# Decay-argument matmuls on 128 rows, and the C-B diagonal in one VectorE instruction

## The chip, the cores and the metric

The kernel runs on one core of a Trainium2 chip. The metric is the device time of one execution in microseconds (us). The profile shows the engines TensorE (PE for matmuls, PEld for the loads of their stationary operand), VectorE (DVE), ScalarE (ACT), GpSimd (POOL) and SyncE (SP), whose queue issues all DMAs here.

## The reference

One layer of a hybrid mixer over 2048 latent tokens of width 1024, with 256 context tokens as a prefix. What matters here is the state-space (SSD) group: 24 heads of 64 channels in 4 groups of 6 heads, a state of 128, chunks of 128 tokens, scanned in both directions.

```python
def ssd_chunked(x, dt, A, B, C, h0):
    ...
    xc = (x * dt[..., None]).reshape(bsz, nc, CHUNK, g, r, p)
    a = (dt * A).reshape(bsz, nc, CHUNK, g, r).transpose(0, 3, 4, 1, 2)
    a_cum = jnp.cumsum(a, axis=-1)
    lmat = jnp.exp(segsum(a))          # exp(a_cum[l] - a_cum[s]) for s <= l
    cb = jnp.einsum('bclgn,bcsgn->bgcls', cc, bc)
    y_diag = jnp.einsum('bgcls,bgrcls,bcsgrp->bclgrp', cb, lmat, xc)
    ...
    y_off = jnp.einsum('bclgn,bcgrpn,bgrcl->bclgrp', cc, prev_states, jnp.exp(a_cum))
    y = (y_diag + y_off).reshape(bsz, length, g, r, p)
...
y = y_f + flip(y_b) + d_skip.astype(f32).reshape(g, r)[:, :, None] * xs
gated = y.reshape(bsz, length, g, r * p) * jax.nn.silu(zs.astype(f32)).reshape(bsz, length, g, r * p)
gated = gated * lax.rsqrt(jnp.mean(gated * gated, axis=-1, keepdims=True) + EPS)
out = gated.reshape(bsz, length, D_SSD).astype(zs.dtype) * norm_w
```

## The kernel before

Projections, convolutions, the context scan, the backward scan and the Fourier group come first; they write their results to DRAM. The last stage, which the change is in, then makes the output. It runs over 64 units u: a chunk c of 128 tokens (16 of them) and a group g of 6 heads (4 of them). A unit has six steps, called for different units in one loop turn.

- s1 loads and makes the decay weights. For each direction dr, the exponent of all 6 heads comes from a matmul (L965) of a stationary tile l, which holds 12 rows of log dt minus cumulated decay (6 heads, a high and a low part) and 2 rows of ones, with a moving tile r, which holds 12 rows that select a head and 2 rows of the cumulated decay. These 14 rows start at partition 0 for dr = 0 and at 32 for dr = 1. The output parg has 128 x 384 elements, for three heads; there are two halves, h2 = 0 and 1. VectorE merges the two directions with a mask (copy_predicated, L967), ScalarE takes exp into w (L969), and VectorE multiplies w by C-B (cb, L970). A parg tile has two PSUM buffers.
- The matmul pcb (L947) gives C-B for the group; ScalarE copies it to cb. VectorE takes its diagonal: times the identity (cbi, L951), then a sum along the row (cbd, L953), and from it the scale dsc (L956) of the term that ScalarE makes in six instructions (xd, L1012). pcb shares one PSUM buffer with pn.
- s2 loads the states and makes the off-chunk output (pyo, L1005 to L1007), from high and low parts sh and sl; s3 advances the forward state hf (pst, L1031 to L1033, and L1036, L1037).
- s4 multiplies x by w (py, L1046, 64 output columns a head) and adds ts by transposes into the same PSUM tile (L1049); s5 makes the group's norm (pn, L1062, and L1065 to L1071); s6 multiplies by the output weights (po, L1105 to L1107) and, for the last group of a chunk, makes the residual and the final norm.

All engines have queues in order. The order of the instructions is set by a scheduler that simulates the program with costs of its own; it need not be the order of the source. Two tiles r (rt) take turns, and three tiles l (lt). Their constant rows are written once, before the stage; per unit SP loads the 2 rows of cumulated decay of r and the 12 rows of l, for each direction.

Of the kernel before, what the change touches and what calls it, by code (L numbers as in the profile page):

```python
# [9 lines left out]
F32 = mybir.dt.float32  # L10
F32R = mybir.dt.float32r
U8 = mybir.dt.uint8
AF = mybir.ActivationFunctionType
ALU = mybir.AluOpType
AX = mybir.AxisListType
# [3 lines left out]
P = 128  # L19
# [9 lines left out]
HG = 6  # L29
# [20 lines left out]
def mixer_layer(ctx: ExitStack, tc: tile.TileContext, A: dict, out: bass.AP, taps=None):  # L50
    nc = tc.nc
    mm = nc.tensor.matmul
# [9 lines left out]
    def load(dst, src):  # L62
        return nc.sync.dma_start(out=dst, in_=src).ins
# [3 lines left out]
    def copy(dst, src):  # L67
        return nc.scalar.activation(dst, src, AF.Copy).ins  # L68
# [21 lines left out]
    q_d = scratch("q_d", [2, W2, SEQ], F32R)  # L90
# [807 lines left out]
    msk32 = wa1.tile([P, HG, P], F32, name="st1", tag="w")[:, 0]  # L898
    load(msk32, A["msk"])
    nc.vector.tensor_copy(out=msk, in_=msk32)  # L900
    LR = 46
    rt = [wa1.tile([LR, HG * P], F32R, name=f"rt{i}", bufs=1) for i in range(2)]
    lt = [wa1.tile([LR, P], F32R, name=f"lt{i}", bufs=1) for i in range(3)]
    for t in rt:
        st1 = wa1.tile([P, HG, P], F32, name="st1", tag="w")
        load(st1[:LR], A["rrows"].rearrange("r (h w) -> r h w", w=P))
        copy(t, st1[:LR].rearrange("r h w -> r (h w)"))
    for t in lt:
        nc.vector.tensor_copy(out=t, in_=ones[:LR, :])

    for n in range(4):
        out_weights(n, lambda sh: W["p"].tile(sh, F32, name="wo", tag="raw", bufs=1), 1)
# [10 lines left out]
    def s1(u):  # L923
        c, g = divmod(u, G)
        d = units[u] = {}
        if g == 0:
            sml = wa1.tile([P, 4, W2], F32, name="sml4", tag="sml")
            load(sml, sm_d[c])
        else:
            sml = units[u - 1]["sml"]  # L930
        d["sml"] = sml
        r, l = rt[u % 2], lt[u % 3]
        cs = slice(c * P, c * P + P)
        for dr in range(2):
            hsl = slice(dr * H + g * HG, dr * H + (g + 1) * HG)
            load(r[32 * dr + 12:32 * dr + 14, :].rearrange("o (h w) -> o h w", w=P).bitcast(F32),
                 cum_d[:, hsl, cs].bitcast(F32))
            for s in range(2):
                load(l[32 * dr + 6 * s:32 * dr + 6 * s + 6, :].bitcast(F32), q_d[s, hsl, cs].bitcast(F32))
        bc = wa1.tile([P, 2, P], F32, name="bc", tag="bc", bufs=2)  # L940
        load(bc, bcT_d[c, :, g])
        d["bc"] = bc
        chl = wa1.tile([P, 2, P], F32R, name="chl", tag="chl")
        load(chl[:].bitcast(F32), chl_d[c, :, g].bitcast(F32))
        d["chl"] = chl
        pcb = ps.tile([P, P], F32, name="pcb", tag="misc", bufs=1)
        mm(pcb, bc[:, 0], bc[:, 1], start=True, stop=True)  # L947
        cb = wa1.tile([P, P], F32, name="cb", tag="cb")
        copy(cb, pcb)
        cbi = wa1.tile([P, P], F32, name="cbi", tag="cbi", bufs=1)  # L950
        nc.vector.tensor_tensor(out=cbi, in0=cb, in1=ident, op=ALU.mult)  # L951
        cbd = wa1.tile([P, 1], F32, name="cbd", tag="cbd")
        nc.vector.tensor_reduce(out=cbd, in_=cbi, axis=AX.X, op=ALU.add)  # L953
        dsc = wa1.tile([P, HG], F32, name="dsc", tag="dsc")
        hs = slice(g * HG, (g + 1) * HG)
        nc.vector.scalar_tensor_tensor(out=dsc, in0=sml[:, 3, H + g * HG:H + (g + 1) * HG], scalar=cbd[:, 0:1],  # L956
                                       in1=dsk[:, hs], op0=ALU.mult, op1=ALU.add)
        d["dsc"] = dsc
        w = wa1.tile([P, HG, P], F32, name="w", tag="w")
        for h2 in range(2):  # L960
            cols = slice(384 * h2, 384 * h2 + 384)
            pa = []
            for dr in range(2):
                po = ps.tile([P, 3, P], F32, name="parg", tag="arg", bufs=2)
                mm(po, l[32 * dr:32 * dr + 14, :], r[32 * dr:32 * dr + 14, cols], start=True, stop=True)  # L965
                pa.append(po)
            nc.vector.copy_predicated(out=pa[0], mask=msk[:].unsqueeze(1).broadcast_to([P, 3, P]), data=pa[1])  # L967
            with tc.issue_after(pre2):
                d["exp"] = nc.scalar.activation(w[:, 3 * h2:3 * h2 + 3], pa[0], AF.Exp).ins  # L969
        nc.vector.tensor_tensor(out=w, in0=w, in1=cb[:].unsqueeze(1).broadcast_to([P, HG, P]), op=ALU.mult)  # L970
        d["w"] = w
# [225 lines left out]
def shape_constants():  # L1197
    f = lambda a: np.ascontiguousarray(a, dtype=np.float32)
    K = {}
    i = np.arange(P)  # L1200
    K["ident"] = f(np.eye(P))
    K["sel"] = f(np.tile(np.eye(32)[:, :2], (4, 1)))
    K["i2"] = f(np.concatenate([np.eye(2 * H), np.eye(2 * H)], axis=0))
    K["ones"] = f(np.ones((P, P)))
    K["triu"] = f(i[:, None] <= i[None, :])
    K["tril"] = f(i[:, None] >= i[None, :])
    K["msk"] = f(i[None, :] < i[:, None])
    rr = np.zeros((46, HG * P))
    for base in (0, 32):
        for s in range(2):  # L1210
            for h in range(HG):
                rr[base + 6 * s + h, h * P:(h + 1) * P] = 1.0
    K["rrows"] = f(rr)
    n1 = np.arange(P)
    m1 = np.zeros((P, P))
    for k1 in range(64):
        t, k1l = divmod(k1, 4)
        m1[:, 2 * k1l * 16 + t] = np.cos(2 * np.pi * ((k1 * n1) % P) / P)
        m1[:, (2 * k1l + 1) * 16 + t] = -np.sin(2 * np.pi * ((k1 * n1) % P) / P)
    m1[:, 16] = np.cos(np.pi * n1)  # L1220
    K["dft1"] = f(m1)
    scale = 1.0 / math.sqrt(SEQ * 64.0)
    n2 = np.arange(16)
    k2 = np.arange(16)
    tw = np.zeros((16, 8, 16, 2, 16, 4))
    for t in range(16):
        for k1l in range(4):
            k1 = 4 * t + k1l
            th = 2 * np.pi * ((n2[:, None] * (k1 + P * k2[None, :])) % SEQ) / SEQ
            tw[t, 2 * k1l, :, 0, :, k1l] = np.cos(th)  # L1230
            tw[t, 2 * k1l, :, 1, :, k1l] = -np.sin(th)
            if k1 > 0:
                tw[t, 2 * k1l + 1, :, 0, :, k1l] = np.sin(th)
                tw[t, 2 * k1l + 1, :, 1, :, k1l] = np.cos(th)
    K["tw"] = f((tw * scale).transpose(0, 2, 1, 3, 4, 5).reshape(16, P, P).transpose(1, 0, 2))
    t64 = np.zeros((8, 16, 2, 16))
    th = 2 * np.pi * ((n2[:, None] * (64 + P * k2[None, :])) % SEQ) / SEQ
    t64[1, :, 0, :] = np.cos(th)
    t64[1, :, 1, :] = -np.sin(th)
    K["tw64"] = f((t64 * scale).transpose(1, 0, 2, 3).reshape(P, 32))  # L1240
    j = np.arange(64)
    th = 2 * np.pi * ((j[:, None] * j[None, :]) % 64) / 64
    for name, m in (("c64", np.cos(th)), ("s64", np.sin(th))):
        b = np.zeros((P, P))
        b[:64, :64] = m
        b[64:, 64:] = m
        K[name] = f(b)
    return K
# [15 lines left out]
```

## Time and profile before

| | us |
|---|---|
| Median of 3 runs | 1965.88 |
| Lowest and highest | 1959.27, 1967.3 |
| Span of the profiled execution, first to last instruction | 1965.1 |
| PE matmul busy in it | 1885.8 |
| DVE busy | 1478.9 |
| ACT busy | 890.0 |
| POOL busy | 809.4 |

The profile gives the profiled execution's span, and no time beside it; the span is 0.8 us under the median of the runs. Times of the trace count from the start of the span. Busy shares are averages over stages with different limits, so the stage from about 1215 us to the end is read by itself.

### The profile page before, as it was taken

The numbers are of one execution on the slowest core, as the hardware profiler recorded it, in microseconds if no ns is written. First come the engines' busy times: TensorE is split into PE (matmuls) and PEld (weight loads), VectorE is DVE, ScalarE is ACT, GpSimd is POOL, SyncE is SP. The second block draws the span as 40 slices with busy tenths as digits, with TensorE's granted clock in tenths as the row PEclk, the third lists the DMA queues.
The fourth block names the chain that finished last, engine by engine and source line by source line (L and its number), as shares of the span: only waits on it lengthen the run. The fifth ranks groups of instructions, "written<-read, shape, count | busy, mean of one in ns | idle before, by whom it ended". The sixth has DMA issues, their size and how long they took to land.

```text
span 1965.1 us, 27142 instructions
## 1 busy us (share of the span) xinstructions
PE 1885.8 (96%) x9136; PEld 1499.5 (76%) x9136; DVE 1478.9 (75%) x2083; ACT 890.0 (45%) x2008; POOL 809.4 (41%) x635
## 2 busy tenths in 40 slices
PE   6999999999999999999889999999999999999998
PEld 2799988878888788888677787667777677777776
DVE  3743298998988995338896136998999899999885
ACT  2631144444444443442332433665565555555653
POOL 1321021110201211035573224776777677777663
PEclk8999999999999999999999998879999999999999
DMA  7332132322423323355777547543343333334331
GB/s 267 143 96 77 35 107 60 113 83 66 121 70 89 113 79 101 104 162 189 259 260 235 193 133 230 177 148 118 117 123 115 112 111 120 117 109 129 119 119 37
DMA packets 233132, 253.12 MB, mean 129 GB/s; under 512 B 23269, under 2 KB 194245, under 8 KB 232482
## 3 DMA queue, kind: packets, MB, share of 16 engines
q1 hardware_dynamic: 232994, 251.39, 41.0%
q8 instruction: 73, 1.20, 0.3%
q14 instruction: 65, 0.53, 0.1%
HBM read 165.31 MB, written 86.02 MB: 128 GB/s over the span
## 4 chain that ended last, share of the span: by engine, by line
PE 61%; DVE 23%; DMA 4%; ACT 4%; issue 4%; POOL 3%; SPq 0%; DVEq 0%; ACTq 0%; POOLq 0%
DVE acc L434 10%; PE pj L170 8%; PE pj L169 8%; PE pj L171 8%; PE po L1105 4%; PE po L1107 4%; PE po L1106 4%; PE parg L965 3%; PE py L1046 2%; ACT xd L1012 2%; PE pj L381 2%; PE pj L380 2%; PE pj L379 2%; DVE xl L72 1%; DMA hb_d<-hs 1%
## 5 line engine op out<-in xcount | busy, mean ns | idle before, releaser
L434 DVE SCALAR_TENSOR_TENSOR acc<-img,c_convw,acc 128x1024 f32<-128x1024 f32 x320 | 464.0, 1457 | 59.0 <-ACT acc L431 48.9
L169 PE MATMUL pj<-hh,wh 128*128 128x512 f32 x1152 | 453.1, 397 | 1.2 <-DVE hs L673 1.2
L170 PE MATMUL pj<-hl,wh 128*128 128x512 f32 x1152 | 454.0, 394 | 0.0
L171 PE MATMUL pj<-hh,wl 128*128 128x512 f32 x1152 | 453.1, 393 | 0.0
L72 POOL TENSOR_TENSOR wl<-raw,wh 128x1024 fp32r<-128x1024 f32 x48 | 124.3, 2591 | 590.7 <-ACT wh L68 579.0
L171 PEld LDWEIGHTS pj<-hh,wl 128*128 128x128 f32 x1152 | 217.8, 189 | 45.5 <-issue 0.2
L169 PEld LDWEIGHTS pj<-hh,wh 128*128 128x128 f32 x1152 | 218.6, 190 | 43.9 <-DVE hs L673 1.5
L170 PEld LDWEIGHTS pj<-hl,wh 128*128 128x128 f32 x1152 | 218.3, 190 | 42.0 <-issue 1.8
L1105 PE MATMUL po<-hl,mh 128*128 128x512 f32 x384 | 161.3, 420 | 0.9 <-ACT mh L68 0.4
L1106 PE MATMUL po<-hh,mh 128*128 128x512 f32 x384 | 155.7, 406 | 0.0
L1107 PE MATMUL po<-hl,ml 128*128 128x512 f32 x384 | 150.0, 412 | 0.0
L1012 ACT ACTIVATE xd<-xg,dsc 128x64 f32<-128x64 f32 x384 | 98.7, 336 | 30.8 <-DVE dsc L956 18.8
L1013 POOL TENSOR_TENSOR us<-us,xd 128x384 f32<-128x384 f32 x64 | 68.9, 1076 | 101.8 <-ACT xd L1012 101.4
L965 PE MATMUL parg<-rt,lt 14*128 14x384 f32 x256 | 100.2, 452 | 5.0 <-DMA bc<-bcT_d 4.1
L438 ACT ACTIVATE so<-acc,c_convb 128x1024 f32<-128x1024 f32 x40 | 46.1, 1153 | 129.8 <-DVE acc L434 129.6
L969 ACT ACTIVATE w<-parg 128x384 f32<-128x384 f32 x128 | 62.1, 485 | 88.7 <-DVE parg L967 88.6
L1105 PEld LDWEIGHTS po<-hl,mh 128*128 128x128 f32 x384 | 73.1, 190 | 24.5 <-issue 6.0
L965 PEld LDWEIGHTS parg<-rt,lt 14*128 14x128 f32 x256 | 42.2, 187 | 60.0 <-issue 28.3
L72 POOL TENSOR_TENSOR ml<-gt,mh 128x384 fp32r<-128x384 f32 x64 | 75.6, 1181 | 29.7 <-ACT mh L68 28.6
L641 POOL TENSOR_TENSOR xt<-xt,sml 128x768 f32<-128x768 f32 x38 | 65.7, 1749 | 49.7 <-DMA xt<-xtok_d 31.7
L1106 PEld LDWEIGHTS po<-hh,mh 128*128 128x128 f32 x384 | 73.3, 191 | 15.6 <-issue 2.6
L68 ACT ACTIVATE tk<-ptr 128x512 f32<-128x512 f32 (+1 forms) x80 | 41.9, 549 | 95.1 <-PE ptr L414 91.5
(390 smaller groups left out, 4195.6 us busy)
## 6 DMA issues: line engine op xcount, KB each, us to landing
raw<-in_win SPq DMA_DIRECT2D x48, 512.0 KB
xt<-xtok_d SPq DMA_DIRECT2D x19, 768.0 KB
xtok_d<-tk SPq DMA_DIRECT2D x48, 256.0 KB
zsT_d<-ev SPq DMA_DIRECT2D x48, 256.0 KB
hb_d<-hs SPq DMA_DIRECT2D x16, 768.0 KB
hb<-hb_d SPq DMA_DIRECT2D x64, 192.0 KB
zs<-zsT_d SPq DMA_DIRECT2D x64, 192.0 KB
xg<-xtok_d SPq DMA_DIRECT2D x64, 192.0 KB
```

Source lines behind the costliest of these rows:

```text
L72: (lo_engine or nc.vector).tensor_tensor(out=lo, in0=src, in1=hi.bitcast(F32), op=ALU.subtract)
L169: mm(po, wh[:, k], a, start=(k == 0), stop=False)
L170: mm(po, wh[:, k], b, start=False, stop=False)
L171: mm(po, wl[:, k], a, start=False, stop=(k == KT - 1))
L434: nc.vector.scalar_tensor_tensor(out=acc, in0=im[:, r0 + dy:r0 + dy + 16, dx:dx + GRID_W], scalar=tap(t), in1=acc, op0=ALU.mult, op1=ALU.add)
L641: nc.gpsimd.tensor_tensor(out=xq, in0=xq, in1=wd, op=ALU.mult)
L965: mm(po, l[32 * dr:32 * dr + 14, :], r[32 * dr:32 * dr + 14, cols], start=True, stop=True)
L1012: nc.scalar.activation(xd[:, h], xg[:, h], AF.Copy, scale=d["dsc"][:, h:h + 1])
L1013: nc.gpsimd.tensor_tensor(out=us, in0=us, in1=xd, op=ALU.add)
L1105: mm(po, a, wh[:, i], start=(g == 0 and q == 0), stop=False)
L1106: mm(po, a, wl[:, i], start=False, stop=False)
L1107: mm(po, b, wh[:, i], start=False, stop=(g == 3 and q == 3))
```

## The change

The stationary tile gets 128 rows and a plane for each direction. A plane is zero except for its direction's 14 rows, so the moving tile, also of 128 rows, can hold both directions' rows at once. The matmul then names the whole tiles. The constant rows come from DRAM (rrows with 128 rows, lrows new), and there are two tiles l instead of three. The diagonal is one scalar_tensor_tensor that reads pcb from PSUM, multiplies by the identity and sums into cbd; its product goes to w[:, 0], which exp overwrites.

```diff
-    LR = 46
-    rt = [wa1.tile([LR, HG * P], F32R, name=f"rt{i}", bufs=1) for i in range(2)]
-    lt = [wa1.tile([LR, P], F32R, name=f"lt{i}", bufs=1) for i in range(3)]
+    rt = [wa1.tile([P, HG * P], F32R, name=f"rt{i}", bufs=1) for i in range(2)]
+    lt = [wa1.tile([P, 2, P], F32R, name=f"lt{i}", bufs=1) for i in range(2)]
     for t in rt:
         st1 = wa1.tile([P, HG, P], F32, name="st1", tag="w")
-        load(st1[:LR], A["rrows"].rearrange("r (h w) -> r h w", w=P))
-        copy(t, st1[:LR].rearrange("r h w -> r (h w)"))
+        load(st1, A["rrows"].rearrange("r (h w) -> r h w", w=P))
+        copy(t, st1[:].rearrange("r h w -> r (h w)"))
+    st2 = wa1.tile([P, HG, P], F32, name="st1", tag="w")
+    load(st2[:, :2], A["lrows"])
     for t in lt:
-        nc.vector.tensor_copy(out=t, in_=ones[:LR, :])
+        nc.vector.tensor_copy(out=t, in_=st2[:, :2])
...
-        r, l = rt[u % 2], lt[u % 3]
+        r, l = rt[u % 2], lt[u % 2]
...
-                load(l[32 * dr + 6 * s:32 * dr + 6 * s + 6, :].bitcast(F32), q_d[s, hsl, cs].bitcast(F32))
+                load(l[32 * dr + 6 * s:32 * dr + 6 * s + 6, dr].bitcast(F32), q_d[s, hsl, cs].bitcast(F32))
...
-        cbi = wa1.tile([P, P], F32, name="cbi", tag="cbi", bufs=1)
-        nc.vector.tensor_tensor(out=cbi, in0=cb, in1=ident, op=ALU.mult)
+        w = wa1.tile([P, HG, P], F32, name="w", tag="w")
         cbd = wa1.tile([P, 1], F32, name="cbd", tag="cbd")
-        nc.vector.tensor_reduce(out=cbd, in_=cbi, axis=AX.X, op=ALU.add)
+        nc.vector.scalar_tensor_tensor(out=w[:, 0], in0=pcb, scalar=1.0, in1=ident, op0=ALU.mult, op1=ALU.mult,
+                                       accum_out=cbd)
...
-        w = wa1.tile([P, HG, P], F32, name="w", tag="w")
...
-                mm(po, l[32 * dr:32 * dr + 14, :], r[32 * dr:32 * dr + 14, cols], start=True, stop=True)
+                mm(po, l[:, dr], r[:, cols], start=True, stop=True)
...
-    rr = np.zeros((46, HG * P))
-    for base in (0, 32):
+    rr = np.zeros((P, HG * P))
+    lr = np.zeros((P, 2, P))
+    for d, base in enumerate((0, 32)):
+        lr[base + 12:base + 14, d] = 1.0
...
+    K["lrows"] = f(lr)
```

The scheduler places the stage's instructions anew. On TensorE, in the steady part of the stage, the second half of a unit's parg stood alone between output matmuls, here in before (the numbers in names tell buffers apart):

```order
L1062 MATMUL pn<-s_15709,c_ones 128x128
L965 MATMUL parg<-rt_8979,lt_8983 128x384
L1106 MATMUL po_15725<-hh,mh 128x512
L1107 MATMUL po_15725<-hl,ml 128x512
L1105 MATMUL po_15726<-hl,mh 128x512
L1106 MATMUL po_15726<-hh,mh 128x512
L965 MATMUL parg<-rt_8979,lt_8983 128x384
L1107 MATMUL po_15726<-hl,ml 128x512
```

Now, in one unit of four, all of a unit's parg stand close together, with pcb between the first two and pn between the last two:

```order
L948 MATMUL pcb<-bc 128x128
L965 MATMUL parg<-rt_8980,lt_8982 128x384
L1031 MATMUL pst_15744<-xh_15740,bh_15736 128x384
L1032 MATMUL pst_15744<-xl_15741,bh_15736 128x384
L1033 MATMUL pst_15744<-xh_15740,bl_15737 128x384
L1105 MATMUL po_15637<-hl,mh 128x512
L1106 MATMUL po_15637<-hh,mh 128x512
L1046 MATMUL py<-w,xg 64x128 x6
L1049 MATMUL py<-c_ident,ts 128x128 x3
L965 MATMUL parg<-rt_8980,lt_8982 128x384
L1062 MATMUL pn<-s_15453,c_ones 128x128
L965 MATMUL parg<-rt_8980,lt_8982 128x384
```

The second parg of h2 = 1 and pn have moved nearer to the parg of h2 = 0 and to pcb; in the other units there is more between them.

On VectorE, the diagonal's two instructions stood behind the mask of h2 = 0 (L967), in before:

```order
L967 COPY_PREDICATED parg<-msk_8975,parg 128x384
L72 TENSOR_TENSOR sl_15343<-hf,sh_15342 128x384
L951 TENSOR_TENSOR cbi<-cb,c_ident 128x128
L1119 TENSOR_TENSOR og<-po_14514,gate 128x512
L1009 TENSOR_TENSOR ts<-pyo,sml_15145 128x384
L953 TENSOR_REDUCE cbd<-cbi 128x1
L1052 SCALAR_TENSOR_TENSOR gt<-py,zs_14868 128x384
L1009 TENSOR_TENSOR us<-pyo,sml_15145 128x384
L956 SCALAR_TENSOR_TENSOR dsc<-sml_14539,cbd,c_dskip 128x6
```

Now one instruction (L953) stands there, and dsc follows it sooner:

```order
L967 COPY_PREDICATED parg<-msk_8975,parg 128x384
L953 SCALAR_TENSOR_TENSOR w,cbd<-pcb,c_ident 128x128
L1119 TENSOR_TENSOR og<-po_15040,gate 128x512
L1037 TENSOR_TENSOR hf<-hf,pst_15744 128x384
L72 TENSOR_TENSOR bl_15885<-bt_15703,bh_15884 128x128
L957 SCALAR_TENSOR_TENSOR dsc<-sml_15065,cbd,c_dskip 128x6
```

It stands between the mask and the exp of h2 = 0, since both it and exp write w. In other units one to three other VectorE instructions stand between the mask and it.

## The prediction

> **What bounds the kernel now.** I read the page's busy shares first, then the windows (busy time of each engine in a stretch), then the order of TensorE's starts inside one window, and last the waits.
>
> ```profile
> PE 1885.8 (96%) x9136; PEld 1499.5 (76%) x9136; DVE 1478.9 (75%) x2083; ACT 890.0 (45%) x2008; POOL 809.4 (41%) x635
> ...
> L965 PE MATMUL parg<-rt,lt 14*128 14x384 f32 x256 | 100.2, 452 | 5.0 <-DMA bc<-bcT_d 4.1
> ```
>
> ```profile
> 1215.00:1232.00 17.00, 14.90 (x48) 10.72 (x48) 15.56 (x26) 8.30 (x25) 14.19 (x14) 0.51 0.63 197
> 1242.00:1256.00 14.00, 13.57 (x42) 8.97 (x41) 13.93 (x28) 9.09 (x25) 8.90 (x10) 0.52 0.56 177
> 1294.00:1314.00 20.00, 17.52 (x60) 12.02 (x60) 18.64 (x28) 9.93 (x26) 14.15 (x14) 0.50 0.43 136
> ...
> 1600.00:1700.00 100.00, 97.80 (x504) 72.43 (x503) 90.00 (x169) 59.12 (x180) 73.32 (x69) 1.00 0.38 116
> ```
>
> The columns after the window are its length, busy PE, PEld, DVE, ACT and POOL, the granted clock, the DMA share and GB/s. The change acts only from about 1215 us, where the 64 units begin. In the steady part (row 1600:1700) PE is busy 97.8% at full clock and DVE 90.0%, so PE leads and DVE is close behind. In the ramp (three rows of 1215 to 1314) the clock is half, and DVE is busy 92 to 99%: there DVE leads.
>
> But busy PE time is modelled, so I look at the starts:
>
> ```profile
> 1692.33 0.39 PE L1106 MATMUL po<-hh,mh 128*128 128x512 f32 x1
> 1692.56 0.40 PE L1107 MATMUL po<-hl,ml 128*128 128x512 f32 x1
> 1692.80 0.39 PE L1105 MATMUL po<-hl,mh 128*128 128x512 f32 x1
> 1693.12 0.44 PE L965 MATMUL parg<-rt,lt 14*128 14x384 f32 x1
> 1693.49 0.50 PE L1106 MATMUL po<-hh,mh 128*128 128x512 f32 x1
> 1693.83 0.40 PE L1107 MATMUL po<-hl,ml 128*128 128x512 f32 x1
> ...
> 1697.25 0.34 PE L1005 MATMUL pyo<-sh,chl 128*128 128x384 f32 x1
> 1697.43 0.33 PE L1006 MATMUL pyo<-sl,chl 128*128 128x384 f32 x1
> 1697.60 0.34 PE L1007 MATMUL pyo<-sh,chl 128*128 128x384 f32 x1
> ...
> 1698.64 0.44 PE L965 MATMUL parg<-rt,lt 14*128 14x384 f32 x1
> 1699.01 0.88 PE L1046 MATMUL py<-w,xg 128*64 128x128 f32 x12
> ...
> 1701.65 0.38 PE L1062 MATMUL pn<-s,c_ones 128*128 128x128 f32 x2
> 1701.96 0.44 PE L965 MATMUL parg<-rt,lt 14*128 14x384 f32 x2
> 1702.34 0.73 PE L1107 MATMUL po<-hl,ml 128*128 128x512 f32 x2
> 1702.90 0.39 PE L1105 MATMUL po<-hl,mh 128*128 128x512 f32 x1
> ```
>
> The step from one full 128x512 matmul to the next is 0.23 us, and 0.17 to 0.18 us for 128x384. Around a 14-row matmul it is not: 0.32 into it (0.09 more), 0.37 out of it (0.20 more than a full 384), and 0.34 for the first step behind it (0.11 more). From 1692.80 to 1693.83 that is 1.03 us where two 512 steps and a full 384 would take 0.64: an isolated parg costs 0.39 us beyond its work. Two in a row (1701.96, x2) run together, in the 0.44 us of one.
>
> ```profile
> ACT w L969 <- DVE parg L967: 67.4, 48, 4.4
> ...
> PEld parg L965 <- issue: 19.9, 70, 0.4
> ...
> DVE parg L967 <- PE parg L965: 7.1, 6, 1.7
> PE pyo L1005 <- DVE hf L1037: 7.0, 6, 1.5
> ...
> PE py L1046 <- DVE w L970: 3.6, 4, 0.9
> ```
>
> In the waits of 1400 to 1900 us (total us, times, longest), the load of parg's weights stands 19.9 us waiting for nothing that another engine does, while PE's real waits for DVE are 7.0 and 3.6 us of 500. So steady PE is bound by its own issue, and the switch to and from 14 rows is part of it. The Trainium skill, "TensorEngine Tiling (Array Packing)", section Key Properties, says that changing the tiling mode drains the array. The 0.39 us above agrees.
>
> **The change, part by part.**
>
> *Full rows.* From the order of before: 256 parg, of which 41 follow another parg directly and 211 follow a full matmul; behind them stand 179 full matmuls and 36 of the 64-column py. The sum: 211 entries x 0.09 = 19.0 us; 179 exits x 0.30 (0.39 less the entry) = 53.7; 36 exits into py, which narrows the array itself and keeps its own switch, x 0.10 = 3.6; and 41 seconds of a pair, which cost nothing today and will cost 0.17, minus 7.0. That is 69 us. In the order of after the py matmuls stand in 64 runs, not 80: 16 switches fewer at 0.3 (my estimate from parg's exit) add 5. PE's work falls by 74 us, 1.16 us a unit. The padded rows cost nothing in the step, by the rows of L1005 to L1007, which are full and take 0.17.
>
> A rule speaks against this. The pair at 1701.96 takes the time of one, so a pair costs one entry and one exit, 0.39, and padding it gains only 0.39 less the 0.17 of its second matmul: 0.22, or 28 us if all 128 pairs stood together. The order has 41, so I stay with 74. The Trainium skill, "TensorE: Matmul & The Clock Gate", Part 3, states it as a rule: small-K matmuls in different row groups run at the same time. The pair agrees.
>
> *DVE's diagonal.*
>
> ```profile
> L970 DVE TENSOR_TENSOR w<-w,cb 128x768 f32<-128x768 f32 x45 | 49.6, 1102 | 9.2 <-ACT w L969 9.1
> L951 DVE TENSOR_TENSOR cbi<-cb,c_ident 128x128 f32<-128x128 f32 x45 | 30.3, 673 | 0.0
> L1056 DVE TENSOR_REDUCE s<-sq 128x128 f32<-128x384 f32 x45 | 26.5, 589 | 10.8 <-ACT sq L1054 6.2 <-PE po L1106 4.4
> L1068 DVE SCALAR_TENSOR_TENSOR tt<-pn,tt 128x128 f32<-128x128 f32 x45 | 12.7, 282 | 4.2 <-ACT tt L1067 4.2
> L953 DVE TENSOR_REDUCE cbd<-cbi 128x1 f32<-128x128 f32 x45 | 12.3, 274 | 0.3
> L119 DVE TENSOR_SCALAR rm<-sso 128x1 f32<-128x1 f32 x12 | 1.8, 151 | 0.3
> ```
>
> These are DVE's groups of 1400 to 1900 us, 45 units (L970 x45), so a unit is 500/45 = 11.1 us and DVE's share of it 10.0. L951 and L953 go: 673 + 274 = 947 ns. No row shows a DVE instruction with an accumulator. Its nearest row is L1068, the same operation on 128x128 with one input in PSUM: 282 ns is the floor; the ceiling adds the reduce it replaces, 282 + 274 = 556. I take 0.45, L1068 plus a one-column DVE instruction (L119, 151): DVE loses 0.50 us a unit (0.39 to 0.67). The Trainium skill, "VectorE: DVE Perf Modes", section Two Vector instructions with no wait between them, counts an accumulator output as a second instruction; no run here shows it on DVE.
>
> *New waits.*
>
> ```profile
> L967 DVE COPY_PREDICATED parg<-msk,parg 128x384 f32<-128x384 uint8 x89 | 49.1, 551 | 7.1 <-PE parg L965 7.1
> ```
>
> ```profile
> L969 ACT ACTIVATE w<-parg 128x384 f32<-128x384 f32 x89 | 43.3, 486 | 67.6 <-DVE parg L967 67.4
> ```
>
> The instruction writes w[:, 0] as waste, so exp of the first half (L969), which fills the same columns, now waits for it as well as for L967, and behind exp stand ACT's copies that feed PE. And pcb's single PSUM buffer, shared with pn, is held until DVE has read it, not only ACT. In the order the instruction stands one to four DVE rows behind L967, so exp comes 0.5 to 2 us later. I cost it at nothing on the path: L969 waits 1.4 us each time (67.4 in 48) as it is, and L970 takes its result several rows later. Where that cover fails, the second parg of h2 = 1 waits, and PE with it.
>
> *lt: three buffers to two.* rt had two already, so the loads of both wait for the same parg; SP's queue holds nothing new behind them. *Staging.* rrows with 128 rows and lrows are 0.63 MB more (2 x 82 rows x 3 KB and 0.13 MB).
>
> ```profile
> 1100.00:1200.00 100.00, 99.59 (x499) 81.73 (x498) 28.29 (x54) 33.78 (x60) 26.21 (x16) 1.00 0.54 166
> ```
>
> They are loaded in that stretch, where PE is 99.6% busy with other work and the DMA engines 54%: 3.8 us at 166 GB/s, hidden; at worst all of it lands in front of unit 0.
>
> *Sum.* PE alone would need 11.1 - 1.16 = 9.95 us a unit, its present waits included. DVE needs 10.0 - 0.5 = 9.5 busy; with its present idle time of 1.1 it would be 10.6, but part of that idle time is waiting for PE (L967, 7.1 us; part of L1056's 10.8). The two now stand almost level, and neither queue will be full. I take 10.3, the middle. From 1314 us to the end are (1965 - 1314)/11.1 = 58 units, less the last one's tail: 57 x 0.8 = 46 us. The 7 of the ramp gain DVE's 0.5 each: 3.5 us. 1965.1 - 50 = 1915 for the span; the runs' median of 1965.88 is 0.8 above the profiled span, so 1916 us.
>
> **Rivals.**
> - *PE stays the only bound.* The low waits on DVE speak for it, DVE at 9.5 of 9.95 us against. 74 us less, and more where denser work ends the half clock of the ramp: 51 us at 0.5 cost up to 25. So 1892, with the clock 1867.
> - *DVE is the bound with today's idle time:* 10.6 us a unit, 57 x 0.5 + 3.5 = 32 us, 1934.
> - *Slower: exp waits for the diagonal.* The place is the order shown above, where the second parg of h2 = 1 stands some 2.6 us behind the last of h2 = 0 (three 384 steps, two 512, py 0.88, parg 0.17, transposes and pn 0.3 each, by pn's step at 1701.65). Of it parg itself, L967, the new instruction and exp need 0.34 + 0.55 + 0.45 + 0.49 = 1.83. It decides once DVE is late by so much that each unit loses more than the 0.8 us; if exp waits another 1.4 us a unit, as L969 does now, and it all falls on PE, 64 x 0.6 = 38 us are lost: 2004. Against it: only one unit in four is so tight, and PE hardly waits for L969 now.
> - *Padding does nothing,* because the 0.39 us belong to parg's operands (late loads, PSUM) and not to its rows. Then only DVE's saving is left where DVE leads: 3.5 us in the ramp and a few beyond, 1955 to 1962. Against it: the step out of parg is 0.37 behind po at 1693 and 0.38 behind pn at 1702, too alike for a late load.
>
> **How the numbers follow.** Mine (10.1 to 10.5 us a unit, 1905 to 1928) 0.50; DVE-bound, 1928 to 1945, 0.17; PE alone, under 1905, 0.16; padding does nothing 0.08; slower or lost to exp's wait 0.09, half of it beyond 1976. The range leaves out the clock's whole gain, the empty change and the slow case: 1890 to 1945. A measurement of this kernel tells about 0.5% (10 us) from no change. Faster is 0.83 and a part of the last two; same the most of the empty change: 0.87, 0.08 and 0.05 for slower.
>
> **What would show it.** In the profile after: steps into and out of parg of 0.23 and 0.17 us, its duration near the 0.34 of L1005, and no "issue" wait of its weights; L953 at 0.3 to 0.5 us; steady windows with DVE at 91 to 95% and a unit of 10.3 us; ACT's wait before exp no longer than now. I am wrong if parg's steps stay, if PE's waits for pn, py or parg grow past 0.5 us a unit, or if the half clock of the ramp lasts longer.

## The result, and the profile after

The changed kernel takes 1978.3 us (median of 4 runs, 1976.4 to 1983.3) against 1964.9 of the kernel before (4 runs, 1959.3 to 1967.3). The ratio is 1.0081, 95% interval 1.006 to 1.0103: slower by 0.8%. The profiled execution's span is 1981.4 us. Two of the four executions of e2 below ran slow, at a lower granted clock (0.93 for 0.94), and its row has the other two alone.

From the page after, the busy times and the groups that answer to those of before:

```profile
PE 1848.8 (93%) x9136; PEld 1510.2 (76%) x9136; DVE 1447.8 (73%) x2082; ACT 882.0 (45%) x2008; POOL 822.4 (42%) x635
...
L1105 PE MATMUL po<-hl,mh 128*128 128x512 f32 x384 | 160.1, 417 | 21.2 <-ACT mh L68 19.7
...
L965 PE MATMUL parg<-rt,lt 128*128 128x384 f32 x256 | 96.8, 390 | 17.1 <-DVE parg L967 10.9
```

PE is busy 37 us less and DVE 31 us less, and the kernel is longer. Both edits did to their engines what they say, and the saving went into waiting: po now waits 19.7 us for ACT's mh, and parg 10.9 us for DVE's mask (L967). In the page before, po waited 0.4 us for mh, and parg 5.0 in all:

```profile
L1105 PE MATMUL po<-hl,mh 128*128 128x512 f32 x384 | 161.3, 420 | 0.9 <-ACT mh L68 0.4
```

TensorE's starts around a padded parg (start, duration, instruction):

```profile
1607.04 0.33 PE L1032 MATMUL pst<-xl,bh 128*128 128x384 f32 x1
1607.21 0.34 PE L1033 MATMUL pst<-xh,bl 128*128 128x384 f32 x1
1607.38 0.34 PE L965 MATMUL parg<-rt,lt 128*128 128x384 f32 x1
1607.56 0.39 PE L1105 MATMUL po<-hl,mh 128*128 128x512 f32 x1
1607.79 0.39 PE L1106 MATMUL po<-hh,mh 128*128 128x512 f32 x1
...
1612.21 0.38 PE L1062 MATMUL pn<-s,c_ones 128*128 128x128 f32 x2
...
1616.28 0.44 PE L1031 MATMUL pst<-xh,bh 128*128 128x384 f32 x1 [0.61 <-DVE us L1009]
...
1618.16 0.80 PE L1105 MATMUL po<-hl,mh 128*128 128x512 f32 x1 [1.09 <-ACT mh L68]
1618.75 0.63 PE L1106 MATMUL po<-hh,mh 128*128 128x512 f32 x1
1619.31 1.55 PE L1046 MATMUL py<-w,xg 128*64 128x128 f32 x12
```

The step into parg is 0.17 and out of it 0.18 us, as between full matmuls (0.32 and 0.37 before). The last rows show a new wait, and DVE's rows of the same time show the other side of it:

```profile
1609.33 0.86 DVE L957 SCALAR_TENSOR_TENSOR dsc<-sml,cbd,c_dskip 128x6 f32<-128x6 f32 x1
1612.70 0.60 DVE L1056 TENSOR_REDUCE s<-sq 128x128 f32<-128x384 f32 x1 [2.51 <-PE pn L1062]
1613.22 0.68 DVE L1119 TENSOR_TENSOR og<-po,gate 128x512 f32<-128x512 f32 x1
```

From 1607.56 PE works through a block of po; pn stands behind it and starts at 1612.21. The tile s has one buffer, so DVE's next s waits for pn, 2.51 us with nothing to do, and all of its work behind s is late by that. Then it is PE's turn: it waits for us (0.61) and for mh (1.09), which comes from DVE's gt. The two engines take turns.

DVE's groups of 1400 to 1900 us after:

```profile
L970 DVE TENSOR_TENSOR w<-w,cb 128x768 f32<-128x768 f32 x44 | 56.9, 1293 | 0.0
...
L957 DVE SCALAR_TENSOR_TENSOR dsc<-sml,cbd,c_dskip 128x6 f32<-128x6 f32 x44 | 35.2, 799 | 0.3
...
L1056 DVE TENSOR_REDUCE s<-sq 128x128 f32<-128x384 f32 x43 | 25.7, 597 | 48.5 <-PE pn L1062 26.6 <-ACT sq L1054 22.0
...
L953 DVE SCALAR_TENSOR_TENSOR w<-pcb,c_ident 128x128 f32<-128x128 f32 x44 | 12.2, 277 | 0.0
...
L953 DVE DVE_READ_ACCUMULATOR w<-pcb,c_ident 128x1 f32 x44 | 3.4, 78 | 0.0
```

The diagonal takes 277 + 78 = 355 ns, for 947 before. DVE idles 48.5 us ahead of s (L1056), 10.8 before.

The waits of the same stretch (total us, times, longest):

```profile
ACT mh L68 <- DVE gt L1071: 92.5, 34, 4.2
...
DVE s L1056 <- PE pn L1062: 26.6, 11, 3.2
DVE fm L72 <- ACT fm L68: 26.1, 10, 3.4
ACT w L969 <- DVE w L953: 22.6, 14, 2.2
...
PEld pn L1062 <- DVE w L953: 9.8, 11, 1.1
```

Both new waits of the change are there: exp for the diagonal (22.6 us of 500) and pn for the buffer that the diagonal holds (9.8). The question for the experiments is whether they cost the time, or the order that came with them.

For a unit's time I take a window of 40 units, from the start of DVE's L970 of the 17th to that of the 57th. Columns: length, busy PE, PEld, DVE, ACT, POOL, granted clock. Before, then after:

```profile
1420.29:1865.15 444.86, 435.95 (x2238) 322.22 (x2236) 403.04 (x748) 261.13 (x797) 324.04 (x300) 1.00 0.38 117
```

```profile
1411.59:1873.29 461.70, 422.45 (x2239) 331.95 (x2239) 383.16 (x751) 257.10 (x801) 332.04 (x299) 0.98 0.38 114
```

By 40: a unit took 11.12 us, DVE 10.08 busy and 1.05 idle. Now it takes 11.54, with 9.58 and 1.96.

### The profile page after: what moved, and what is told of

It reads as the page before. It is cut to its first block, busy times and chain, and to the rows that moved or that the text cites. A ratio compares the mean times of both kernels' runs of the same rounds, so it can differ in the third digit from the quotient of the medians.

```text
span 1981.4 us, 27052 instructions
## 1 busy us (share of the span) xinstructions
PE 1848.8 (93%) x9136; PEld 1510.2 (76%) x9136; DVE 1447.8 (73%) x2082; ACT 882.0 (45%) x2008; POOL 822.4 (42%) x635
## 4 chain that ended last, share of the span: by engine, by line
PE 54%; DVE 30%; DMA 5%; ACT 4%; issue 4%; POOL 1%; SPq 1%; DVEq 0%; ACTq 0%; POOLq 0%
DVE acc L434 10%; PE pj L170 8%; PE pj L169 8%; PE pj L171 8%; PE po L1105 4%; PE po L1106 4%; PE po L1107 4%; DMA hb_d<-hs 2%; DVE w L970 2%; DVE xl L72 2%; PE pj L381 2%; PE pj L380 2%; PE pj L379 2%; PE py L1046 1%; DVE hs L671 1%
## 5 line engine op out<-in xcount | busy, mean ns | idle before, releaser
L1105 PE MATMUL po<-hl,mh 128*128 128x512 f32 x384 | 160.1, 417 | 21.2 <-ACT mh L68 19.7
L965 PE MATMUL parg<-rt,lt 128*128 128x384 f32 x256 | 96.8, 390 | 17.1 <-DVE parg L967 10.9
L72 POOL TENSOR_TENSOR ml<-gt,mh 128x384 fp32r<-128x384 f32 x64 | 68.4, 1069 | 84.4 <-ACT mh L68 81.9
L68 ACT ACTIVATE mh<-gt 128x384 fp32r<-128x384 f32 x64 | 33.4, 522 | 120.2 <-DVE gt L1071 117.1
L72 POOL TENSOR_TENSOR sl<-hb,sh 128x384 fp32r<-128x384 f32 x64 | 81.5, 1273 | 11.9 <-ACT sh L68 11.8
L1107 PEld LDWEIGHTS po<-hl,ml 128*128 128x128 f32 x384 | 71.7, 191 | 17.9 <-POOL ml L72 4.3
```

Of the source, the lines that this page charges most:

```text
L72: (lo_engine or nc.vector).tensor_tensor(out=lo, in0=src, in1=hi.bitcast(F32), op=ALU.subtract)
L965: mm(po, l[:, dr], r[:, cols], start=True, stop=True)
L1105: mm(po, a, wh[:, i], start=(g == 0 and q == 0), stop=False)
L1107: mm(po, b, wh[:, i], start=False, stop=(g == 3 and q == 3))
```

## The experiments

Ratios are to the kernel before, run beside each. The scheduler places the stage anew for every edit, so some kernels hold PE, DVE, ACT and POOL to a given order by a table of numbers ("old order" is that of the kernel before); SP's loads are then free, but in e10 and e14 they are held too.

| | median us | ratio, 95% |
|---|---|---|
| e1 padding alone | 1967.5 | 1.0025, 1.0015 to 1.0035 |
| e2 diagonal alone | 2065.9 | 1.0532, 1.0511 to 1.0553 |
| e3 both, neither new wait | 1956.4 | 0.9966, 0.9951 to 0.9981 |
| e4 both, PSUM buffer held, w not | 1961.9 | 0.9989, 0.9976 to 1.0002 |
| e15 both, w's wait alone | 1976.2 | 1.0063, 1.0046 to 1.008 |
| e5 padding, no diagonal | 1951.1 | 0.9946, 0.9926 to 0.9965 |
| e6 14 rows, no diagonal | 1976.3 | 1.0056, 1.0038 to 1.0074 |
| e7 padding, parg twice | 1992.1 | 1.0142, 1.0122 to 1.0162 |
| e8 padding, diagonal on POOL and PE | 1954.7 | 0.9956, 0.9937 to 0.9974 |
| e17 before, bc held, old order | 1968.4 | 1.0028, 1.0014 to 1.0042 |
| e9 padding, old order | 1966.8 | 1.0028, 1.0015 to 1.004 |
| e10 14 rows in e1's order | 1979.0 | 1.0086, 1.0066 to 1.0107 |
| e11 both, w not waiting, old order | 1947.5 | 0.9922, 0.9899 to 0.9944 |
| e12 padding, no diagonal, old order | 1929.3 | 0.9836, 0.9817 to 0.9855 |
| e13 14 rows, no diagonal, old order | 1943.0 | 0.9898, 0.9878 to 0.9917 |
| e16 padding, diagonal on POOL and ACT, old order | 1964.6 | 1.0001, 0.999 to 1.0011 |
| e14 e4 in the change's order, loads too | 2006.3 | 1.0218, 1.02 to 1.0236 |
| e18 e4 in the change's order, loads free | 1984.7 | 1.0103, 1.0087 to 1.012 |

### One edit at a time: e1 and e2

e1 takes the padding and keeps the old pair; its product goes over the half of bc that pcb has read:

```diff
+        cbi = bc[:, 0]
+        nc.vector.tensor_tensor(out=cbi, in0=cb, in1=ident, op=ALU.mult)
...
-        nc.vector.scalar_tensor_tensor(out=w[:, 0], in0=pcb, scalar=1.0, in1=ident, op0=ALU.mult, op1=ALU.mult,
-                                       accum_out=cbd)
+        nc.vector.tensor_reduce(out=cbd, in_=cbi, axis=AX.X, op=ALU.add)
```

> The padding alone: parg with 128 rows and lt with two buffers, the diagonal by the old pair (multiply, reduce), with the product laid into bc[:, 0] for want of SBUF. Theory 1 (the one-instruction diagonal's new waits eat the gain): parg's step stays at 0.17 us, no wait of exp for L953, pn waits for nothing on DVE; DVE is as busy as before (10.0 us a unit), so the unit is 10.6 to 10.9 us and the time 1920 to 1945. Theory 2 (any new order of the stage is worse than the tuned one): 1960 to 1985 here too, with PE about 93% busy in the steady part and ACT's ml and mh late. Theory 3 (lt with two buffers): as theory 2, but the waits end on lt's loads.

e2 is the other half: the one instruction, and parg at 14 rows with three lt.

> The diagonal alone: one instruction on pcb with its product in w[:, 0], parg left at 14 rows. Theory 1 (its waits cost): PE keeps the 0.39 us of each isolated parg and gets the new waits as well: 1990 to 2030, with s L1056 waiting for pn and pn for L953. Theory 2 (the order alone, whichever edit sets it): 1965 to 1985, like both edits. Theory 4 (the padding costs something not yet seen and the diagonal helps): 1945 to 1960.

Padding alone gains nothing, where theory 1 wanted 20 to 45 us. The diagonal alone costs 5.3%, more than either theory said. Between e2 and the change, both with the new diagonal, lie 1.0532 - 1.0081 = 4.5%, 88 us; but each of these kernels has an order of its own, so that is no measure of the padding alone. Forty units of e2:

```profile
1428.20:1946.97 518.77, 489.24 (x2240) 355.95 (x2240) 387.58 (x752) 262.65 (x800) 323.89 (x301) 0.89 0.34 101
```

A unit is 13.0 us there, at a granted clock of 0.89, against 11.54 us and 0.98 in the change. How PE's waits and its clock go together is shown in the last section.

### The two new waits: e3, e4 and e15

These differ in two arguments of the one instruction:

```diff
e3   out=bc[:, 0], in0=cb     (neither wait)
e4   out=bc[:, 0], in0=pcb    (pcb's PSUM buffer held until DVE has read)
e15  out=w[:, 0],  in0=cb     (exp waits for it, and it for w's buffer)
```

> Both edits without the two new dependencies: the one instruction reads cb (the copy in SBUF) and lays its product into bc[:, 0], so exp does not wait for it and pcb's PSUM buffer is free once ACT has copied it. Theory 1: no pn wait on DVE, unit 10.3 to 10.6 us, 1910 to 1935. Theory 2: 1960 to 1985.

> Both edits with one of the two new dependencies: the one instruction reads pcb in PSUM (the buffer shared with pn is held until DVE has read it), its product goes to bc[:, 0], so exp does not wait for it. Theory 1a (the held PSUM buffer is what costs): as slow as both edits, 1965 to 1985, with pn waiting for L953 and s L1056 for pn. Theory 1b (exp's wait is what costs): as without both dependencies, 1910 to 1935. Half and half: 1940 to 1955.

> Both edits, the one instruction reading cb in SBUF (so pcb's PSUM buffer is free after ACT's copy) with its product in w[:, 0] (so exp waits for it, and it for w's buffer), in the scheduler's own order. If w's wait and the order it forces are what makes the change slower: 1970 to 1985. If it takes both dependencies together: 1955 to 1965.

The held PSUM buffer costs little (e4 against e3: 0.2%). Writing to w costs 1.0% (e15 against e3) or 0.9% (the change against e4), the new order that comes with it included. But e3 and e4 lie in the ranges of neither theory: even without both waits, e3 is 21 to 46 us slower than theory 1 expected. About a third of the miss goes with these waits and the orders that came with them (1978 - 1956 of 1978 - 1916); two thirds are elsewhere.

### Is DVE or PE the bound: e5, e6, e7, e8

e5 and e6 leave the diagonal out, with and without padding:

```diff
+        cbd = ones
```

> The padding with no diagonal at all: dsc takes the constant 1 in place of the diagonal, so the term of the skip weight is left out of the right size, and VectorE loses 0.95 us a unit against the padding alone. Theory A (PE and VectorE are both almost full in the kernel before, so taking work from one pays nothing until the other is relieved too): the unit falls from 11.1 to 10.2 to 10.5 us, 1905 to 1930. Theory B (neither is full: a chain of waits through the queues, in the order that the scheduler sets, holds the unit): 1945 to 1960, with VectorE's share of the steady windows near 83% and PE's near 94%.

> No diagonal (dsc takes the constant 1), and parg left at 14 rows: the same 0.95 us a unit taken from VectorE, but PE keeps its switches. Theory A: PE holds the unit near 11.0 us, so 1950 to 1962; the gain with the padding (the run before this) is much larger than the sum of the two alone. Theory B: the gain here is as large as there, whatever it is.

e7 issues each padded parg a second time into the same tile:

```diff
                 mm(po, l[:, dr], r[:, cols], start=True, stop=True)
+                mm(po, l[:, dr], r[:, cols], start=True, stop=True)
```

> The padding alone (old diagonal), with each parg matmul issued twice into the same tile: 4 x 0.17 = 0.68 us of full-row matmul a unit put back on PE, about the same as the switches that the padding took away, without any switch. Theory A: PE has that much slack once padded, so the time is that of the padding alone, 1962 to 1972, and the short stretches of half clock in the steady part go, since PE is busier. Theory B, or PE still the bound: each unit is longer by 0.3 to 0.7 us, 1985 to 2005.

e8 makes the diagonal off DVE:

```diff
+        nc.gpsimd.tensor_tensor(out=w[:, 0], in0=bc[:, 0], in1=bc[:, 1], op=ALU.mult)
+        mm(pcb[:, P:P + 1], w[:, 0], ones[:, 0:1], start=True, stop=True)
```

> The padding, with the diagonal off VectorE altogether and in full: POOL multiplies the two halves of bc (into w[:, 0], as soon as bc is loaded), a one-column matmul with ones sums it into column 128 of pcb's tile, and ACT's copy of cb brings it along. VectorE loses 0.95 us a unit, POOL gains 0.4 to 0.7, PE 0.1. Theory A: 1915 to 1940. Theory B: 1945 to 1965. If POOL's multiply comes late (POOL is 70% busy and waits in its queue), pcb and cb come late with it and the time is over 1970.

All four spoke against theory A as stated; e5, e7 and e8 lie in the ranges of theory B, and e6 fits neither. It leaves out 0.95 us of DVE's work a unit and is slower, 1.0056; e13 below, the same kernel in the old order, takes 0.9898, so it was the order. e7 puts 4 x 0.17 x 64 = 44 us back on PE and takes 1992.1 - 1967.5 = 25 more, but in another order again, so it doesn't show whether PE had slack. The half clock that was to go by theory A stayed (mean granted clock 0.98 in e7's 40 units). So the order had to be held still.

### The order held: e9, e10, e17

A table puts each engine's queue in the order of the kernel before (e9, e17) or of e1 (e10):

```diff
+        pin(tc)
```

> The padding alone, with PE, DVE, ACT and POOL held to the order of the kernel before (a table pins each queue; SP's loads are free, since with two tiles lt the old order of the loads cannot be kept). Theory of the order (the scheduler, which places everything anew for any edit, gave the padded kernel a worse order, and that took what the padding saved): 1915 to 1935. Theory of the loop (in whatever order, a chain of waits between PE, DVE and ACT holds the unit near 11.1 us, and PE has slack): 1955 to 1970, as in the scheduler's own order (1967).

> The other half of the exchange: the kernel before, with 14 rows and three lt, every queue held to the order that the scheduler gave the padding alone. Theory of the order: the padding's saving is missing and the order is worse, 2000 to 2040. Theory of the loop: 1965 to 1980.

> A control: the kernel before, 14 rows and the old diagonal pair, in the old order, with the product laid into bc[:, 0] and SP's loads free, as in the padding alone in the old order (e9, 1967). If these two cost nothing: 1960 to 1967, and the padding is worth nothing while VectorE keeps the diagonal. If they cost what padding saved: 1980 to 2010.

The padding is worth nothing in the old order too: 1.0028 with it (e9) and 1.0028 without it (e17), all else alike. In e1's order it is worth 1.0086 - 1.0025, 0.6% (e10 has a tile of its own for the product, where e1 uses bc). e9 and e10 lie in the ranges of the loop. Forty units of e9:

```profile
1418.75:1862.37 443.62, 411.71 (x2235) 329.89 (x2233) 408.47 (x749) 257.90 (x797) 325.35 (x300) 0.99 0.39 117
```

PE's busy time falls from 10.90 to 10.29 us a unit, and the unit stays at 11.09. DVE is busy 10.21 of it. The waits of e9 say where PE's time went:

```profile
PEld pyo L1006 <- DVE hf L1038: 17.2, 11, 1.8
PE pyo L1006 <- DVE hf L1038: 14.7, 11, 1.5
...
PE py L1047 <- DVE w L971: 8.1, 10, 1.3
```

These were 7.0 (pyo) and 3.6 us (py) before. PE is done sooner and waits for DVE.

### DVE relieved, in the old order: e11, e12, e13

e11 has both edits with the product in bc[:, 0], the diagonal where the multiply stood. e12 and e13 leave the diagonal out, with padding and with 14 rows.

> Both edits in the order of the kernel before, the one diagonal instruction standing where the multiply stood, reading pcb from PSUM, its product in bc[:, 0]. (With the product in w[:, 0] the old order cannot be had: the queues would wait for each other in a circle, because w's buffer is then needed before py of two units earlier has run.) Theory of the order: as the padding in the old order, and up to 30 us less, since VectorE is relieved by 0.58 us a unit: 1890 to 1925. Theory of the loop: 1945 to 1965.

> The padding without a diagonal (dsc takes the constant 1) in the order of the kernel before: a bound for all that taking work from VectorE can bring there. Theory of the order: 1880 to 1915, at or a little under both edits in that order; PE's busy share back above 96%. Theory of the loop: 1945 to 1960.

> 14 rows, no diagonal (dsc takes the constant 1), in the order of the kernel before. Theory of two bounds (PE with its switches and VectorE with the diagonal each hold the unit near 11 us): 1945 to 1960, so less than half of the 33 us that the same removal gives with padding (e12). Theory of VectorE alone (PE never was the bound): as e12, 1925 to 1940. Theory of PE alone: no gain, 1960 to 1966.

The reason that e11's expectation gives for w[:, 0] is not the one that the traces show. In the kernel before, py of two units earlier had always ended when the multiply (L951) started, so w's buffer was free. What stands in the way is that exp would wait for the diagonal. Here are ACT's and then DVE's rows of the tenth unit before, exp being that of the first half:

```profile
1323.87 0.47 ACT L969 ACTIVATE w<-parg 128x384 f32<-128x384 f32 x1
1324.24 0.51 ACT L1054 ACTIVATE sq<-gt 128x384 f32<-128x384 f32 x1
```

```profile
1325.40 0.58 DVE L1056 TENSOR_REDUCE s<-sq 128x128 f32<-128x384 f32 x1
1326.83 1.35 DVE L951 TENSOR_TENSOR cbi<-cb,c_ident 128x128 f32<-128x128 f32 x1
```

The multiply stands behind s, s reads sq, and sq stands behind exp (L969): if exp waits for the diagonal in the multiply's place, neither queue can go on. The 13th unit has such a pair too, with bh and bl. In the other units none was found, so whether an order close to the old one would do with the product in w isn't tested.

Forty units of e11, e12 and e13:

```profile
1410.54:1842.13 431.59, 401.43 (x2236) 325.20 (x2235) 385.45 (x749) 259.70 (x797) 319.26 (x298) 1.00 0.40 120
```

```profile
1407.77:1830.53 422.76, 404.01 (x2238) 331.90 (x2237) 377.58 (x669) 257.91 (x797) 318.00 (x299) 0.98 0.41 123
```

```profile
1417.50:1845.45 427.95, 427.37 (x2230) 319.16 (x2229) 371.06 (x669) 262.36 (x796) 314.84 (x300) 1.00 0.41 122
```

| old order | unit | DVE busy | DVE idle | PE busy |
|---|---|---|---|---|
| before | 11.12 | 10.08 | 1.05 | 98.0% |
| padding (e9) | 11.09 | 10.21 | 0.88 | 92.8% |
| both (e11) | 10.79 | 9.64 | 1.15 | 93.0% |
| padding, no diagonal (e12) | 10.57 | 9.44 | 1.13 | 95.6% |
| 14 rows, no diagonal (e13) | 10.70 | 9.28 | 1.42 | 99.9% |

Held in one order, the unit is DVE's busy time and 0.9 to 1.15 us in which it waits for the others, but for e13. There PE is full, at 10.70: the same matmuls in the same order, with their switches, need no more than that, not 11.1. So in the kernel before it was DVE with its waits that set the unit, and PE's 98% hid at least 0.4 us a unit of slack. The four kernels of e9, e12, e13 and e17 show both bounds: against the kernel before, leaving out the diagonal brings 1.0% at 14 rows and 1.6% with padding; padding brings nothing with the diagonal and 0.6% without. Of the sizes that were expected of the theory of the order none was met: e11 lies in the loop's range, e12 between the two, and e13 between two bounds and VectorE alone. e11, which computes everything, is faster than both kernels, by 0.8% (0.6 to 1.0) and 1.6%.

e16 was to get e12's time with the diagonal in full:

```diff
+        nc.gpsimd.tensor_tensor(out=cbi, in0=cb, in1=ident, op=ALU.mult)
+        nc.scalar.activation(cbi, cbi, AF.Copy, accum_out=cbd)
```

> The padding, with the diagonal in full but off VectorE: POOL multiplies cb by the identity into bc[:, 0], ACT sums the row with its accumulator; the old order, the new instructions where the scheduler wants them. If VectorE is the bound that is left: close to the run without any diagonal (1929), 1928 to 1942. If POOL's and ACT's added 0.5 to 0.7 us a unit each come late for dsc and xd: 1945 to 1965.

It did not: 1964.6, as its second expectation has it, and the waits fit that:

```profile
DVE dsc L957 <- ACT bc L954: 21.5, 24, 1.8
...
ACT bc L954 <- POOL bc L952: 11.1, 10, 2.0
```

DVE's busy time fell to 9.5 us a unit, but dsc now waits for ACT, which waits for POOL.

### The wait or its order: e14 and e18

Both take e4, without w's wait, and hold it to the order of the change as it is.

> Both edits with the product in bc[:, 0], so that exp does not wait for the diagonal and the diagonal does not wait for w's buffer, but every queue held to the order of the change as it is. If the order costs: 1972 to 1982, like the change (1978). If the wait itself costs: 1955 to 1965, like the same kernel in its own order (1962).

> Both edits without w's wait, with PE, DVE, ACT and POOL in the order of the change as it is and SP's loads free. If the order costs: 1972 to 1985, like the change. If the wait itself costs: 1950 to 1965, like the same kernel in its own order.

In e14 the loads' queue was held as well, and the one row that stands out is an artefact of the longer held bc:

```profile
SPq L63 <- DVE bc L953: 100.0, 33, 5.7
```

It tells nothing of w. e18 does. It has no wait of exp for the diagonal, and is as slow as the change (1.0103; less the 0.0028 of e17, which holds bc in the old order, 1.0075, for the change's 1.0081). So the order costs, and not the wait. e11, e4 and e18 are one source in three orders: the old one, the scheduler's own and the change's. Forty units of e4 and e18:

```profile
1406.68:1854.60 447.92, 424.95 (x2242) 332.83 (x2242) 375.10 (x751) 262.81 (x801) 319.17 (x300) 0.98 0.39 117
```

```profile
1415.45:1881.82 466.37, 427.95 (x2239) 338.78 (x2239) 384.75 (x751) 257.99 (x801) 332.84 (x301) 0.96 0.38 113
```

The unit is 10.79 us in e11, 11.20 in e4 and 11.66 in e18, and the ratios are 0.9922, 0.9989 and 1.0103.

What in the order costs is only in part to be seen. The DVE groups of s in 1400 to 1900 us, e18 and then e4:

```profile
L1057 DVE TENSOR_REDUCE s<-sq 128x128 f32<-128x384 f32 x42 | 25.0, 596 | 44.3 <-PE pn L1063 23.5 <-ACT sq L1055 20.8
L1057 DVE TENSOR_REDUCE s<-sq 128x128 f32<-128x384 f32 x45 | 26.7, 594 | 43.8 <-PE pn L1063 43.8
```

e18 has 44 us of idle DVE ahead of s, near the 48.5 of the change. In the steady part of before, pn stands 9 to 16 rows behind pcb in PE's order (a row is a run of equal instructions); in the change it stands 7 to 10 rows behind it in one unit and 25 to 28 in the next, with the block of po between, and s waits for it. But e4 idles 43.8 us there too and is no slower than the kernel before, so this wait alone doesn't explain the change's time. What e4 lacks is the wait of DVE for ACT's fm, 26.1 us in the change and 28.7 in e18. No run tests one of these waits by itself.

## Why the prediction was wrong, by its own steps

- **Full rows, and "So steady PE is bound by its own issue".** The price of the switch was right: the steps around a padded parg are 0.17 and 0.18 us, with no issue wait of its weights. The conclusion failed. e9 takes the switches away and the unit stays at 11.09 us; e13 shows that PE needed at most 10.70 us a unit with them. DVE and its waits set the 11.1, so work taken from PE alone could bring nothing. The sum of 74 us is not shown by any total: PE's busy time fell by 10.90 - 10.29 = 0.61 us a unit in e9, 39 us in 64 units. Busy time doesn't tell all, since a matmul that is followed by a wait counts there for its whole 0.33 us and one that is followed by another for the step of 0.17. The 0.10 us for an exit into py was taken from no row; at 3.6 us in all it decides nothing. The rival "padding does nothing" had the size of the padding alone (no change), but not the cause: the switches did belong to the 14 rows, and their time turned into waits for DVE.
- **DVE's diagonal.** I took 0.45 us, it is 0.355, and the profile lists two DVE instructions for it, as the Trainium skill, "VectorE: DVE Perf Modes", section Two Vector instructions with no wait between them, has it. The saving of 0.50 us a unit came out right, 10.08 - 9.58 = 0.50 in the change and 10.08 - 9.64 = 0.44 in e11, but by luck: by the durations it was 0.947 - 0.355 = 0.59. More than half of the multiply's 673 ns was a wait for POOL (276 ns at the least, last section), and part of such a wait moves on to other instructions. Leaving the diagonal out took 0.64 (e12) and 0.80 us (e13) from DVE's busy time, not 0.95.
- **New waits, "I cost it at nothing on the path", and no term for a new order.** The exp's wait was small, as said: in 500 us exp waited 67.4 for L967 before, and 22.6 for the diagonal and 0.3 for L967 after; and e18, without it, is no faster. But the sum takes its unit and its idle times from the order of before, and of the order of after only py's runs. This step turned a gain into a loss: e11 to e4 is 0.7% (from the old order to the scheduler's own), e4 to the change 0.9% (to the order that the scheduler made with the write to w), together 31 us.
- **lt and staging.** At nothing, and nothing speaks against it: e9 has both, with the padding, and e17 neither, at the same ratio, and no wait of e9 in 1400 to 1900 us ends on a load of lt. The stretch of 1100 to 1200 us after has PE busy 99.4%.
- **Sum.** "I take 10.3, the middle" stood between 9.95, which rested on PE, and 10.6. With the order held it is 10.79, near the rival that DVE is the bound with today's idle time (10.6, 1934). In the change's order it is 11.54. As ratios, the forecast is 1916 / 1965.9 = 0.975 and the change 1.008. About half of the 3.3% between them, 1.8%, lies between the forecast and e11, and goes to the belief that PE was the bound; the 0.7 and 0.9% of the orders are the rest. Even e11, at 1947.5, is over the 1945 of the range.
- **The ramp.** DVE was to give 0.5 us for each of 7 units. In the window 1215 to 1314 us DVE is busy 92.43 us before and 91.72 after, and L970 of the ninth unit starts at 1319.0 and 1319.8 us; no gain.
- **The slower rival** had the right side and the wrong place: exp waits 22.6 us in 500 for the diagonal, but e18 loses the same without it.
- **The signs of being wrong** that were named did not appear: parg's steps went, PE's own waits at parg, py and pn after are 8.0, 6.1 and 6.1 us of 500, together just under 0.5 us a unit, and the half clock of the ramp got shorter (mean granted clock of 1215 to 1314 us 0.74 before, 0.83 after). What did show was the other end of the list: DVE is busy 83% of the 40 units, not 91 to 95%, and the unit is 11.54 us, not 10.3.

What stays open: why the scheduler's order is worse in some versions than in others (e1 to e9 nothing, e4 to e11 0.7%, e5 to e12 1.1%, e6 to e13 1.6%), which would need its own costs beside the measured ones; which wait of the change's order costs most; and whether the product can go to w in a better order.

## What to carry to other kernels

Two engines above 90% can both look like the bound; hold the order still and take work from one of them, since a busy matmul time is modelled and hides slack (98% here, and 0.4 us of 11.1 free). An edit that lets a scheduler place a stage anew changes two things at once, the work and the order, and the order was worth more here: 1.8% between three orders of one source, where the two edits brought 0.8% in the old order. A place to throw a product away is not free: it ties the instruction to the other writers of that buffer, and that can forbid the exact order that the kernel was good in.

## What the runs showed of the hardware

The diagonal's multiply in the kernel before, and dsc, by tile (min, median, max ns):

```profile
L951 DVE TENSOR_TENSOR cbi<-cb,c_ident x45: 276/641/1372, 1399.2 to 1892.3; 128x128 f32<-128x128 f32 x45
```

```profile
L956 DVE SCALAR_TENSOR_TENSOR dsc<-sml,cbd,c_dskip x45: 208/356/991, 1401.0 to 1894.9; 128x6 f32<-128x6 f32 x45
```

```profile
L1009 DVE TENSOR_TENSOR us<-pyo,sml x45: 540/544/558, 1401.7 to 1893.3; 128x384 f32<-128x384 f32 x45
```

The same instruction takes 276 ns or 1372. Of 44 multiplies, the 4 with less than 0.05 us of POOL's work beside them took 278 ns in the mean, the other 40 took 701. Of 45 dsc, the 15 with less than 0.05 us of POOL's work beside them took 214 ns in the mean, the other 30 took 519. The last row reads PSUM with one input and never varies. The Trainium skill, "SBUF — State Buffer", section SBUF: two separate sides, says that VectorE with two SBUF inputs and GpSimd share a pair of ports, which one of them holds for a whole instruction. These rows agree. After the change dsc is 799 ns in the mean, 418 before, and L970 1293, 1102 before; in the old order (e11) they are 513 and 1077. So how much of the multiply's wait comes back in other instructions depends on the order.

Short waits of PE went with a loss of clock. In the change's rows of 1614.6 to 1625 us:

```profile
1614.60:1618.00 3.40, 1.79 (x8) 1.02 (x7) 3.40 (x6) 2.83 (x9) 2.51 (x3) 1.00 0.44 128
1618.10:1621.50 3.40, 3.34 (x18) 2.36 (x19) 3.40 (x8) 0.49 (x2) 3.40 (x4) 0.50 0.12 42
1621.60:1625.00 3.40, 3.40 (x19) 2.94 (x18) 2.52 (x5) 2.79 (x11) 2.21 (x3) 1.00 0.45 134
```

A stretch of 3.4 us in which PE was busy 1.79 is followed by one of the same length at half the granted clock, in which py takes 1.55 us for 0.88. The Trainium skill, "TensorE: Matmul & The Clock Gate", Part 1, gives a window of 3.4 us after which an idle array's clock is halved; here the array was not idle but half busy. From 1400 to 1890 us the change has five such stretches of half clock, and in the 3.4 us before each PE was busy 47 to 56%; one of 57%, from 1450.8 us, was not followed by half clock. In e12 stretches of 62 to 63% were, so the share is no sharp limit. The steady part of the kernel before has no such stretch, by its granted clock of 1.00.
